# A hybrid decoder trunk on one core: the first two token blocks of the shared key projection move from the transposes' PSUM banks to the accumulator's

## The chip, the cores and the metric

The kernel runs on one core of one Trainium2 chip. The metric is the time of one execution on the device in microseconds (us), lower is better. The core's engines are PE (matrix products and transposes), DVE and POOL (vector work), ACT (activations and copies) and SP, which issues most of the transfers. Each engine works through its own queue in order. An instruction that waits for another engine holds up everything behind it on its queue.

## The reference, cut to what matters

The program computes a two-layer decoder trunk for one sequence of 512 tokens and a model width of 1024, in float32. Layer 0 has native sparse attention beside memory attention, and a squared-ReLU MLP. After it, keys and values are projected once from the residual stream. Layer 1 has dilated sliding-window attention over these keys and values beside memory attention, an output projection, and a second MLP. Cut to the part around the change:

```python
x = x + squared_relu_mlp(rmsnorm(x, mlp_norm[0]), w_up[0], w_down[0])   # end of layer 0
k_s, v_s = jnp.split(rmsnorm(x, kv_norm) @ w_kv_shared, 2, axis=-1)      # 512 x 1024 times 1024 x 1024
k_shared = rope(rmsnorm(split_heads(k_s, 8), kv_k_norm), pos)
v_shared = split_heads(v_s, 8)
q, q_mem = jnp.split(rmsnorm(x, attn_norm[1]) @ b_w_in[0], [B_Q], axis=-1)
o_main = dilated_attention(q, k_shared, v_shared, b_q_norm[0])           # three patterns, merged
o_mem = memory_attention(q_mem, mem_kv, mem_q_norm[1], mem_k_norm[1])
x = x + jnp.concatenate([o_main, o_mem], axis=-1) @ b_w_out[0]
```

## The kernel before, in words

**Products.** Each float32 operand is split into a high and a low part, so each product is three matmuls: high by high (L260), high by low (L261), low by high (L262). A pair of weight tiles is loaded into a staging buffer (pool `st`, 3 buffers) by a transfer on SP. ACT then copies the high part to a buffer of pool `w` (L253, 4 buffers), and DVE or POOL makes the low part by a subtraction (L255).

**PSUM.** The eight banks are four pools (L186): `acc` with 2 banks, `ps` with 3, `pt` with 2 and `po` with 1. A tile taken from a pool waits until the instructions that read the tile that had this bank before it are done. Names in the trace and in the order begin with the pool: `s_acc_6795` is a tile of `acc`, with its number.

**End of layer 0's MLP.** The last quarter of the MLP accumulates products in pairs of banks and adds them into the result `xn` (a tile of the SBUF pool `pt4`, shown as s_pt) with DVE (L216, in `into`). The last two steps are `product(X, ...)`, in the two `acc` banks, evicted by `into(X, 0, 0)`, and `product(V, ...)`, in the `pt` banks, evicted by `into(V, 0, 1)`. The result is in rows by tokens. `columns` (L1243 to L1265) turns it: for each half of the token rows and of the columns it takes a `ps` bank, makes four transposes of 128 x 128 per bank on PE (L1251), copies the bank out with ACT (L1258) or DVE (L1256), writes it to DRAM (`xd`), and builds the scaled operand `xk` of the key and value projection from it with ACT (L276) and DVE (L277). Token rows 256 to 511 are turned earlier, rows 0 to 255 in the very end of the MLP.

**Keys and values.** `layer_b` then calls `proj` (L300) for the keys, in the order of the token blocks 2, 3, 0, 1 (128 tokens each), so that the blocks whose operands are there first come first. One block is eight weight tiles by three matmuls of 128 x 512, in one bank. `proj` takes the bank where the block begins; its argument `pool` is one pool for all blocks, or a list that is indexed by the token block:

```python
ps = self.ps(pool[b] if isinstance(pool, list) else pool or self.pacc, [P, n])
```

Each finished key block is normalised on DVE (L513, L1419) and rotated on POOL (L524 to L527, L1423), in two halves. The value blocks follow in `ps` banks, evicted by ACT (L1404) and written to DRAM by POOL (L1405). Then come the query projections of layer B (`proj_b`).

**End of layer B's attention.** Memory attention runs there in four items (scores L657, softmax on ACT at L216, transposes L676, copies L730, values L734), beside the merge of the three dilated patterns (L1661 to L1681). The first part of the output projection, `outpart` (L1115 to L1149), fills the gaps on PE with blocks of nine matmuls into `acc` banks, each with its own weight (transfer from `in_w_bo_dram` to `st`, ACT L253, then L255). Its last part accumulates in `ps` banks when all heads are done.

**What sets the order.** The program text gives a first order. The scheduler of the framework then orders each engine's queue with a simulated timeline of the whole program (`schedule_with_timeline_sim=True`), so a change at one place can alter the order elsewhere.

## Time and profile before

| | |
|---|---|
| Runs | 1295.83, 1298.2 and 1300.5 us, median 1298.2 us |
| Profiled execution, its own time | 1296.08 us |
| Its span | 1294.3 us, 18328 instructions |
| Mean granted clock of PE | 0.995 |
| PE busy | 1244.8 us, 96% of the span |
| DVE, ACT, POOL busy | 825.1, 756.5 and 379.0 us (64%, 58%, 29%) |
| Last MLP matmul before the transposes of rows 0 to 255 | starts at 682.66 us |
| First matmul of the key projection | starts at 688.57 us |

The rows of the timeline that follow give the start and the duration of an instruction, its engine and line, what it writes and reads, the shape and the count; in square brackets stands how long the engine was idle just before it, and what it waited for. All times are counted from the start of the span.

### The profile page before, as it was taken

The numbers are of one execution on the slowest core, as the hardware profiler recorded it, in microseconds if no ns is written. First come the engines' busy times: TensorE is split into PE (matmuls) and PEld (weight loads), VectorE is DVE, ScalarE is ACT, GpSimd is POOL, SyncE is SP. The second block draws the span as 40 slices with busy tenths as digits, with TensorE's granted clock in tenths as the row PEclk, the third lists the DMA queues.
The fourth block names the chain that finished last, engine by engine and source line by source line (L and its number), as shares of the span: only waits on it lengthen the run. The fifth ranks groups of instructions, "written<-read, shape, count | busy, mean of one in ns | idle before, by whom it ended". The sixth has DMA issues, their size and how long they took to land.

```text
span 1294.3 us, 18328 instructions
## 1 busy us (share of the span) xinstructions
PE 1244.8 (96%) x6416; PEld 1021.6 (79%) x6416; DVE 825.1 (64%) x1502; ACT 756.5 (58%) x1684; POOL 379.0 (29%) x478
## 2 busy tenths in 40 slices
PE   9899989899999999999998989998999999999998
PEld 7768777677788888888887888887678888888887
DVE  6846676654656557465588467676657656656566
ACT  6845677774575464554657367777557445355462
POOL 4546665633140010000104689562314000000000
PEclk9999999999999999999999999999999999999999
DMA  7531231334488797887874421210339789697434
GB/s 260 195 119 55 67 126 62 66 74 132 159 252 234 248 238 231 276 237 248 236 212 139 143 74 51 71 42 9 108 126 291 219 271 243 211 287 218 151 110 163
DMA packets 61837, 215.28 MB, mean 166 GB/s; under 512 B 6736, under 2 KB 14928, under 8 KB 61232
## 3 DMA queue, kind: packets, MB, share of 16 engines
q1 hardware_dynamic: 50800, 143.72, 33.7%
q0 software_dynamic: 9344, 35.77, 14.0%
q10 hardware_dynamic: 1600, 34.61, 7.4%
q8 instruction: 51, 0.84, 0.3%
q14 instruction: 42, 0.34, 0.1%
HBM read 208.83 MB, written 72.35 MB: 217 GB/s over the span
## 4 chain that ended last, share of the span: by engine, by line
PE 80%; DVE 8%; ACT 6%; POOL 3%; issue 2%; DMA 2%; POOLq 0%; ACTq 0%; DVEq 0%
PE s_ps L261 14%; PE s_ps L262 13%; PE s_ps L260 13%; PE s_acc L260 5%; PE s_acc L261 5%; PE s_acc L262 5%; PE s_po L734 3%; PE s_pt L261 3%; PE s_pt L262 3%; PE s_pt L260 3%; DVE s_w L255 2%; ACT s_p L216 1%; PE s_ps L1542 1%; PE s_acc L867 1%; PE s_acc L566 1%
## 5 line engine op out<-in xcount | busy, mean ns | idle before, releaser
L255 DVE TENSOR_TENSOR s_w<-s_st,s_w 128x1024 fp32r<-128x1024 f32 (+3 forms) x228 | 272.0, 1197 | 254.7 <-ACT s_w L253 253.7
L253 ACT ACTIVATE s_w<-s_st 128x1024 fp32r<-128x1024 f32 (+4 forms) x260 | 251.3, 970 | 186.8 <-PE s_pt L262 41.1
L260 PE MATMUL s_ps<-s_act,s_w 128*128 128x512 f32 x568 | 222.1, 393 | 1.4 <-ACT s_act L295 1.4
L261 PE MATMUL s_ps<-s_act,s_w 128*128 128x512 f32 x568 | 221.4, 390 | 0.9 <-DVE s_act L1681 0.9
L262 PE MATMUL s_ps<-s_act,s_w 128*128 128x512 f32 x568 | 221.6, 390 | 0.0
L260 PEld LDWEIGHTS s_ps<-s_act,s_w 128*128 128x128 f32 x568 | 106.5, 188 | 25.2 <-ACT s_act L295 3.2
L261 PEld LDWEIGHTS s_ps<-s_act,s_w 128*128 128x128 f32 x568 | 106.7, 188 | 23.3 <-DVE s_act L1681 1.1
L262 PEld LDWEIGHTS s_ps<-s_act,s_w 128*128 128x128 f32 x568 | 106.6, 188 | 21.9
L216 ACT ACTIVATE s_p<-s_ps 128x512 f32<-128x512 f32 x64 | 38.2, 597 | 112.5 <-PE s_ps L262 112.5
L1170 POOL DMA_DIRECT2D sum<-in_w_db_dram x16 | 14.4, 902 | 295.3 <-ACT s_p L216 293.6
L260 PE MATMUL s_acc<-s_w,s_act 128*128 128x512 f32 (+3 forms) x272 | 94.9, 354 | 3.6 <-DVE s_tq L947 2.2
L261 PE MATMUL s_acc<-s_w,s_act 128*128 128x512 f32 (+3 forms) x272 | 95.1, 351 | 2.0 <-POOL s_w L255 1.8
L262 PE MATMUL s_acc<-s_w,s_act 128*128 128x512 f32 (+3 forms) x272 | 93.7, 350 | 0.0
L722 POOL TENSOR_SCALAR s_p<-s_p,s_cr,s_ab 128x128 f32<-128x128 f32 (+3 forms) x96 | 60.3, 664 | 47.9 <-DVE s_cr L1063 26.4
L255 POOL TENSOR_TENSOR s_w<-s_st,s_w 128x512 fp32r<-128x512 f32 (+4 forms) x32 | 54.6, 1706 | 63.6 <-ACT s_w L253 63.5
L216 ACT ACTIVATE s_p<-s_ps,s_nm 128x256 f32<-128x256 f32 (+3 forms) x128 | 65.5, 523 | 9.6 <-DVE s_nm L1043 2.8
L730 ACT ACTIVATE s_pt<-s_pt 128x512 f32<-128x512 f32 (+2 forms) x101 | 52.7, 525 | 20.6 <-PE s_pt L1087 8.5
L295 ACT ACTIVATE s_qk<-s_p 128x256 fp32r<-128x256 f32 (+1 forms) x96 | 47.0, 489 | 22.1 <-DVE s_p L1180 20.1
L260 PEld LDWEIGHTS s_acc<-s_w,s_act 128*128 128x128 f32 x272 | 51.7, 191 | 9.7 <-DVE s_tq L947 1.5
L1170 POOL DMA_DIRECT2D sum<-sum x16 | 14.1, 884 | 147.1 <-DMA sum<-sum 38.4
L261 PEld LDWEIGHTS s_acc<-s_w,s_act 128*128 128x128 f32 x272 | 51.9, 191 | 6.3 <-POOL s_w L255 2.4
L262 PEld LDWEIGHTS s_acc<-s_w,s_act 128*128 128x128 f32 x272 | 51.9, 191 | 3.6
(328 smaller groups left out, 2942.3 us busy)
## 6 DMA issues: line engine op xcount, KB each, us to landing
s_st<-in_w_up_dram SPq DMA_DIRECT2D x64, 512.0 KB, 4.1
s_st<-sum SPq DMA_DIRECT2D x64, 512.0 KB, 6.7
s_st<-in_w_db_dram SPq DMA_DIRECT2D x48, 512.0 KB, 4.5
sum<-in_w_db_dram POOLq DMA_DIRECT2D x16, 1024.0 KB, 13.9
sum<-sum POOLq DMA_DIRECT2D x16, 1024.0 KB, 10.9
s_st<-in_w_bq_dram SPq DMA_DIRECT2D x16, 384.0 KB, 3.1
s_st<-in_w_ag_dram SPq DMA_DIRECT2D x11, 512.0 KB, 3.9
s_w<-in_w_c_dram SPq DMA_DIRECT2D x8, 512.0 KB, 5.0
```

Source lines behind the costliest of these rows:

```text
L216: return lambda *a, **k: self.marks.append(f(*a, **k))
L253: nc.scalar.activation(w[:, 0], st, AF.Copy)
L255: e.tensor_tensor(out=w[:, 1], in0=st, in1=w[:, 0], op=ALU.subtract)
L260: mm(ps, lh[0], rh[0], start=start, stop=False, skip_group_check=again)
L261: mm(ps, lh[0], rh[1], start=False, stop=False, skip_group_check=again)
L262: mm(ps, lh[1], rh[0], start=False, stop=stop, skip_group_check=again)
L295: nc.scalar.activation(dst[:, 0], src, AF.Copy)
L566: nc.tensor.matmul(banks[b], tiles[k // 4][:, k % 4, b * P : (b + 1) * P], w[:, k % 4 // 2, k % 2 * 512 : k % 2 * 512 + 512], start=k == 0 ...
L722: self.nc.gpsimd.tensor_scalar(out=p, in0=p, scalar1=c, scalar2=g, op0=ALU.mult, op1=ALU.mult)
L730: self.turned = self.nc.scalar.activation(dst, src, AF.Copy)
L734: i = self.nc.tensor.matmul(*a, **k)
L1170: self.behind(self.nc.gpsimd.dma_start(t[o], x, accum_op=ALU.add, max_dma_last_dim=4096))
```

## The change

The argument `pool` of the key projection is a list now. Token blocks 2 and 3, which are computed first, take their banks from `acc`; blocks 0 and 1 take theirs from `ps` as before.

```diff
-        drain(self.proj(xk, ins["w_kv"][0], 512, evac_k, pool=self.pS, order=(2, 3, 0, 1)))
+        drain(
+            self.proj(xk, ins["w_kv"][0], 512, evac_k, pool=[self.pS, self.pS, self.pacc, self.pacc], order=(2, 3, 0, 1))
+        )
```

The number of instructions is the same on every engine but for how equal ones in a row are counted. Their order differs in two places. Lines behind the edit have a number that is higher by 2 after the change.

The first place is PE at the end of layer 0's MLP: transposes of the result (s_ps_6743 and 6755 are two of the `ps` banks, c_115 is the identity) and the start of the key projection (block tile 6795 and then 6867). Before:

```order
L1251 MATMUL s_ps_6743<-c_115,s_pt_1081_4072 128x128
L1251 MATMUL s_ps_6755<-c_115,s_pt_1081_4072 128x128
L1251 MATMUL s_ps_6755<-c_115,s_pt_1080_4071 128x128
L1251 MATMUL s_ps_6755<-c_115,s_pt_1081_4072 128x128
L260 MATMUL s_ps_6795<-s_w_6787,s_act_6572 128x512
L261 MATMUL s_ps_6795<-s_w_6787,s_act_6572 128x512
```

And now, from the last product of the first group to the next transpose:

```order
L262 MATMUL s_acc_6795<-s_w_6792,s_act_6589 128x512
L260 MATMUL s_acc_6795<-s_w_6804,s_act_6640 128x512
L260 MATMUL s_acc_6867<-s_w_6787,s_act_6572 128x512
L261 MATMUL s_acc_6867<-s_w_6787,s_act_6572 128x512
L262 MATMUL s_acc_6867<-s_w_6787,s_act_6572 128x512
L1251 MATMUL s_ps_6743<-c_115,s_pt_1080_4071 128x128
L260 MATMUL s_acc_6867<-s_w_6787,s_act_6575 128x512
```

The first product of block 6795 stood behind all sixteen transposes; it stands behind the second of them now, twelve more products of this block and the first three of block 6867 stand ahead of the first transpose into 6743, and the other transposes stand between further products.

The second place is ACT at the end of layer B's attention. There s_w_9754 and s_w_9788 are weights of the filler blocks, s_w_9883 and s_w_9895 weights of the last part of the output projection, and s_p_2185_9772 and s_p_2202_9828 are softmax rows of memory attention. Before:

```order
L253 ACTIVATE s_w_9788<-s_st_9786 128x384
L730 ACTIVATE s_pt_2158_9683<-s_pt_9684 128x2x256
L730 ACTIVATE s_pt_2158_9683<-s_pt_9727 128x2x256
L253 ACTIVATE s_w_9883<-s_st_9881 128x384
L253 ACTIVATE s_w_9895<-s_st_9893 128x384
L216 ACTIVATE s_p_2185_9772,s_su_9770<-s_ps_9764,s_nm_9769 128x256 x2
L730 ACTIVATE s_pt_2192_9795<-s_pt_9796 128x2x256
```

And now:

```order
L730 ACTIVATE s_pt_2158_9683<-s_pt_9684 128x2x256
L730 ACTIVATE s_pt_2158_9683<-s_pt_9727 128x2x256
L253 ACTIVATE s_w_9754<-s_st_9752 128x384
L216 ACTIVATE s_p_2185_9772,s_su_9770<-s_ps_9764,s_nm_9769 128x256 x2
L730 ACTIVATE s_pt_2192_9795<-s_pt_9796 128x2x256
L253 ACTIVATE s_w_9788<-s_st_9786 128x384
L1673 ACTIVATE s_p_2196_9804<-s_pt_9802 128x512
```

The copies of 9883 and 9895 stood ahead of the softmax row 9772 and stand further behind now; the copy of 9754, which stood further ahead, stands directly ahead of it, and that of 9788 behind it.

The third place is PE beside it, where s_acc_9757 and s_acc_9791 are the last two filler blocks of nine matmuls, s_pt_9796 and s_pt_9839 take transposes of softmax rows, and s_pt_9802 and s_pt_9807 belong to the merge. Before, both filler blocks stood wholly ahead of these rows:

```order
L262 MATMUL s_acc_9791<-s_act_9352,s_w_9788 128x512
L1661 MATMUL s_pt_9741<-idr,s_nb_9603 8x128 x4
L676 MATMUL s_pt_9796<-c_115,s_p_2169_9714 128x128 x4
L1669 MATMUL s_pt_9802<-s_p_2176_9746,s_ab_6782 128x512
L1674 MATMUL s_pt_9807<-s_p_2176_9746,s_ab_6782 128x512
L676 MATMUL s_pt_9839<-c_115,s_p_2185_9772 128x128 x4
L734 MATMUL s_po_9733<-s_pt_2128_9582,s_tmp_3258 64x512
```

And now, from the last product of filler 9757:

```order
L262 MATMUL s_acc_9757<-s_act_9352,s_w_9754 128x512
L1671 MATMUL s_pt_9802<-s_p_2176_9746,s_ab_6782 128x512
L1676 MATMUL s_pt_9807<-s_p_2176_9746,s_ab_6782 128x512
L260 MATMUL s_acc_9791<-s_act_8302,s_w_9788 128x512
L261 MATMUL s_acc_9791<-s_act_8302,s_w_9788 128x512
L676 MATMUL s_pt_9839<-c_115,s_p_2185_9772 128x128 x4
L262 MATMUL s_acc_9791<-s_act_8302,s_w_9788 128x512
```

Filler 9757 stands between the transposes of 9796 and the merge now, and filler 9791 around the transposes of 9839.

## The prediction

> **What bounds the kernel now.** I read the first part of the page, then the chain of waits, then the 2-us windows of busy time, then the timelines of the engines around the two places that the change touches. Start with the page:

> ```profile
> span 1294.3 us, 18328 instructions
> PE 80%; DVE 8%; ACT 6%; POOL 3%; issue 2%; DMA 2%; POOLq 0%; ACTq 0%; DVEq 0%
> ```

> Four fifths of the chain that ends last run through PE. So the kernel gets shorter where PE stands still or runs slowly, and only as far as nothing else is late there. The key projection begins in such a place. The windows (us, then busy time of PE, weight loads, DVE, ACT, POOL, then the granted clock, the DMA share and GB/s) show it:

> ```profile
> 682.00:684.00 2.00, 1.92 (x13) 1.48 (x11) 1.65 (x5) 1.97 (x7) 0.00 (x0) 1.00 0.89 322
> 684.00:686.00 2.00, 0.33 (x1) 0.14 (x1) 2.00 (x6) 2.00 (x4) 0.00 (x0) 1.00 0.97 286
> 686.00:688.00 2.00, 0.47 (x2) 0.29 (x3) 2.00 (x4) 2.00 (x5) 0.00 (x0) 1.00 0.23 94
> 688.00:690.00 2.00, 2.00 (x9) 1.72 (x9) 2.00 (x4) 2.00 (x6) 0.00 (x0) 0.60 1.01 238
> 690.00:692.00 2.00, 2.00 (x7) 1.57 (x6) 2.00 (x5) 2.00 (x7) 0.00 (x0) 0.55 0.96 340
> 692.00:694.00 2.00, 2.00 (x10) 1.69 (x9) 2.00 (x7) 2.00 (x7) 0.00 (x0) 1.00 1.03 388
> ```

> From 684 to 688 PE works 0.80 us of 4 while DVE and ACT are full; then it is full, but with a granted clock of 0.60 and 0.55. What it waits for stands in its timeline: the sixteen transposes of the MLP's result (L1251), and behind them on PE's queue the key projection's products (L260 to L262).

> ```profile
> 682.89 1.03 PE L1251 MATMUL s_ps<-c,s_pt 128*128 128x128 f32 x8
> 685.66 0.33 PE L1251 MATMUL s_ps<-c,s_pt 128*128 128x128 f32 x1 [1.74 <-DVE s_pt L216]
> 687.19 0.33 PE L1251 MATMUL s_ps<-c,s_pt 128*128 128x128 f32 x1 [1.19 <-ACT s_x L1258]
> 687.85 1.07 PE L1251 MATMUL s_ps<-c,s_pt 128*128 128x128 f32 x6 [0.34 <-DVE s_pt L216]
> 688.57 0.78 PE L260 MATMUL s_ps<-s_w,s_act 128*128 128x512 f32 x1
> ...
> 691.99 0.39 PE L262 MATMUL s_ps<-s_w,s_act 128*128 128x512 f32 x1
> ...
> 701.06 0.39 PE L260 MATMUL s_ps<-s_w,s_act 128*128 128x512 f32 x1
> ```

> PE waits 1.74, 1.19 and 0.34 us, 3.27 together, for the last MLP evictions and for a transpose bank. The first key product starts at 688.57, 0.86 behind the start of the copy on DVE that empties its bank:

> ```profile
> 680.23 0.75 DVE L216 SCALAR_TENSOR_TENSOR s_pt<-s_acc,r,s_pt 128x512 f32<-128x512 f32 x1
> ...
> 687.71 0.68 DVE L1256 COPY s_x<-s_ps 128x512 f32<-128x512 f32 x1
> ```

> The eviction that reads the MLP's own accumulator (s_acc) for the last time before this starts at 680.23 and takes 0.75. So those banks are empty from about 681 and idle, before the transposes begin. Those are the banks that the change takes.

> **The change part by part.** It adds and removes no instruction. The key products for token blocks 2 and 3 no longer stand behind all transposes: 48 of them (two blocks of eight weight tiles by three products) now stand among the transposes. Nothing else of the program text moves, but the scheduler simulates the whole program, so the order at the end of layer B's attention comes out differently too. I cost both.

> First place, the sum. Before, block 0, the third in order, begins at 701.06, which is 18.17 us behind the first of these transposes (701.06 - 682.89). Full-speed spacing comes from the 40 products between 691.99 and 701.06: 9.07 / 40 = 0.227. The first 8 took 691.99 - 688.57 = 3.42 where 8 x 0.227 = 1.82 would do, so the slow clock costs 1.6. Of the 18.17 us, then: 48 x 0.227 = 10.9 are products, 3.27 are waits, 1.6 is clock, and 2.4 are transposes and their beginnings. With the products between them PE has work at each of the three waits: ten products are there to run while DVE finishes the two L216 and the copy. Six transposes in a row need 688.57 - 687.85 = 0.72, or 0.12 each, so sixteen need 1.9. After the change I get 10.9 + 1.9 = 12.8, and the block begins at 695.7. The gain is 18.17 - 12.8 = 5.4 (5.35, rounded). It is bound by 0 from below (if another input keeps the products back as long as the bank did) and by 5.6 from above (3.27 + 1.6 + all but 1.7 of the transposes' 2.4).

> Are the other inputs there? The weights of the third and fourth pair go through ACT (high part) and DVE (low part), as the next rows show:

> ```profile
> 684.67 1.99 ACT L253 ACTIVATE s_w<-s_st 128x1024 fp32r<-128x1024 f32 x2
> 685.92 1.22 DVE L255 TENSOR_TENSOR s_w<-s_st,s_w 128x1024 fp32r<-128x1024 f32 x1
> 688.31 1.22 DVE L255 TENSOR_TENSOR s_w<-s_st,s_w 128x1024 fp32r<-128x1024 f32 x1
> 695.87 0.47 DVE L277 SCALAR_TENSOR_TENSOR s_act<-s_x,gv,s_act 128x256 fp32r<-128x256 f32 x1
> ```

> The low parts are ready at 687.14 and 689.53. By my walk through the new order PE wants the third pair at about 686.3 for its high part (ready at 685.7) and from 687 on for its low part, and the fourth at about 690. No wait is over a few tenths. The last input of the first token rows (L277) ends at 696.34, and those rows are wanted by block 0 alone, its pairs in turn from 695.7 to 701; the last pair is the late one, with over 3 us to spare. So I take 5.3 of 5.4 here.

> Does the gain survive what follows? The keys go through the rotary steps on POOL, and POOL then makes the low parts of the query weights:

> ```profile
> 697.09 0.73 POOL L524 TENSOR_TENSOR s_rb<-s_x,c 128x256 f32<-128x256 f32 x1 [51.58 <-DVE s_r L228]
> ...
> 726.78 0.62 POOL L1423 TENSOR_TENSOR s_x<-s_x,s_r 128x256 f32<-128x256 f32 x1
> ...
> 731.68 1.84 POOL L255 TENSOR_TENSOR s_w<-s_st,s_w 128x768 fp32r<-128x768 f32 x1 [1.61 <-ACT s_w L253]
> 733.70 0.51 PE L260 MATMUL s_ps<-s_w,s_act 128*128 128x384 f32 x2
> ...
> 737.55 0.44 PE L261 MATMUL s_ps<-s_w,s_act 128*128 128x384 f32 x1 [1.23 <-DVE s_w L255]
> ```

> The chain from 697.09 to 727.40 is busy without a break and begins with a DVE step whose place on its queue hardly changes (about 0.5 earlier). It therefore ends at about 726.9, while PE arrives 5.3 earlier. POOL's first weight then would end near 729.3 if it follows right behind the keys; PE took it up at 733.70, so 5.3 earlier it wants it near 728.6, waits about 0.7, and then finds the wait of 1.23 at 737.55 shorter by as much. That nets to nothing, and 5.3 is kept. If the chain were the bound with no such slack, the loss would be all of 5.3; this is the second rival.

> Second place, the end of layer B's attention. Its rows on PE, of the timeline:

> ```profile
> 931.31 0.50 PE L1669 MATMUL s_pt<-s_p,s_ab 8*128 8x512 f32 x1 [0.69 <-DVE s_p L1665]
> 932.68 0.50 PE L1674 MATMUL s_pt<-s_p,s_ab 8*128 8x512 f32 x1 [0.87 <-ACT s_pt L730]
> ...
> 933.98 3.55 PE L734 MATMUL s_po<-s_pt,s_tmp 128*64 128x512 f32 x8
> ...
> 940.20 0.50 PE L261 MATMUL s_ps<-s_act,s_w 128*128 128x512 f32 x1 [0.91 <-DVE s_act L1681]
> ...
> 943.82 1.94 PE L734 MATMUL s_po<-s_pt,s_tmp 128*64 128x512 f32 x8
> 946.46 0.98 PE L260 MATMUL s_ps<-s_act,s_w 128*128 128x512 f32 x3 [0.70 <-ACT s_act L295]
> ```

> Four waits, 0.69 + 0.87 + 0.91 + 0.70 = 3.17. And two groups of eight equal products: 3.55 against 1.94, so 1.6 of clock, which the windows confirm:

> ```profile
> 934.00:936.00 2.00, 2.00 (x7) 0.65 (x8) 0.88 (x4) 2.00 (x8) 1.49 (x2) 0.54 0.16 54
> 936.00:938.00 2.00, 2.00 (x7) 0.51 (x4) 1.07 (x2) 0.69 (x2) 2.00 (x4) 0.61 0.24 62
> ```

> By these it is (1 - 0.54) x 2 + (1 - 0.61) x 2 = 1.7. Together 4.9. The second wait is named for L730, but ACT stood behind a weight that had not landed, with the softmax (L216) queued behind it:

> ```profile
> 928.17 2.45 DMA s_st<-in_w_bo_dram
> 930.71 0.52 ACT L253 ACTIVATE s_w<-s_st 128x384 fp32r<-128x384 f32 x1 [0.73 <-DMA s_st<-in_w_bo_dram]
> 931.14 0.46 ACT L216 ACTIVATE s_p<-s_ps,s_nm 128x256 f32<-128x256 f32 x1
> ```

> In the new order the two copies of output weights that stood ahead of this softmax (9883, 9895) stand behind it, and one that is needed sooner (9754) stands there instead; two filler blocks of nine products stand between the transposes and merges at which PE waited; and four products stand behind the last L734 where PE had waited 0.70 for L295. Walking the new order with the old durations, I get the trio of 946.46 at 940.2, 6.3 earlier, with waits of 0.15 and 0.4 left. The bounds are 6.3 above, and below a small loss, since later copies also free the staging buffers 1.0 to 1.5 later. I take 5, near the 4.9 of the quoted rows, because a walk by hand omits waits that only show when the order runs.

> From 740 to 905 the order on the engines is the same but for a row or so, and what stands there waits for PE, so I carry the shift through at no cost.

> The sum: 5.3 + 5.0 = 10.3, taken as 10. Against the profiled execution, 1296.1 - 10 = 1286.1. That execution lies 2.1 under the median of the runs shown (1298.2), so against the median I expect **1288.2**.

> [...]

> **The rivals.** *Only the first place counts.* For it: the second rests on a walk through an order, and each removed wait there can come back at the next eviction (0.91 at L1681 stays in part). Against: its causes are quoted rows, and the order takes them away. It would give 5.3: 1298.2 - 5.3 = 1293.

> *POOL's key chain takes the first gain back.* For it: the chain has no breaks from 697.09 to 727.40, and the query weights stand behind it. Against: there are 4.3 us between its end and the start at 731.68, and that start waits for ACT. It would leave the 5 of the second place: 1293.

> *The clock terms are not saved.* For it: the dip moves to another idle stretch, as 930 to 934 shows that 1.1 to 1.2 us of work in 2 can be enough. Against: both stretches become full. The gain is 10.3 - 1.6 - 1.7 = 7.0: 1291.

> *Nothing is gained.* The products among the transposes delay the transposes, and so the rows that all 24 products of block 0 need, by as much as PE gained, and the end nets to zero. For it: DVE and ACT are full from 684 to 694, and every window shows 2.00. Against: they work off a backlog that does not hang on PE; the walk leaves over 3 us. 1297 to 1298. That the change doesn't do what it says is excluded by the order, where the products name the accumulator's banks.

> *Slower.* Mechanism: the output weights at the end of the attention become the pacing chain. With three staging buffers, ACT's in-order copies stand at four places ahead of other work (9754, 9788, 9907, 9931), and each is freed 1.0 to 1.5 later than before. The landing there is measured:

> ```profile
> s_st<-in_w_bo_dram SPq DMA_DIRECT2D x13, 192.0 KB, 2.3
> s_st<-sum SPq DMA_DIRECT2D x64, 512.0 KB, 6.7
> ```

> To come out slower by 3.9 it must cost 10.3 + 3.9 = 14.2 over my walk, or 3.6 at each of the four, a landing of 5.9 instead of 2.3. The MLP's slowest class needs 6.7, but for 512 KB. From that point the time is 1302.

> **How the numbers follow.** Both places, near 1288: 0.56. The clock not saved, 1291: 0.12. Only the first place: 0.12. Only the second: 0.07. Nothing: 0.09. Slower: 0.04. A difference of 0.3%, 3.9 us, is about what a measurement of this kernel tells from none. The first four all lie beyond it, though the two at 1293 only by 1.3, of which I count 0.03 as no change: faster 0.84, same 0.12, slower 0.04. The range: below, both upper bounds, 5.6 + 6.3 = 11.9, off the lowest run shown (1295.8) give 1283.9, so 1284; above, the cases at 1293 with 2.3 more, which is the scatter of the runs around their median, 1295.5. About 0.15 is left out.

> **What would show it.** In the changed profile the first key product starts before 685 into an accumulator bank, the 48 run at 0.227 with a clock near 1.00 in the windows from 684 to 694, and block 0 starts near 695.7. If it starts after 697.5, the first term is wrong. POOL's rotary steps still begin near 697, and the wait at the query weights stays under 1 us. At the end of the attention the L1674 wait for L730 is gone, the eight L734 take 1.9, and the trio of three L260 comes about 11 us earlier than 946.46 (5.3 + 6). If ACT's L253 waits for a landing longer than 1 us with L216 behind it, the second term is wrong. A time over 1295.5 would make the whole wrong, since then one of the two gains came back in full.

## The result, and the profile after

The changed kernel takes 1287.74 us in the median of 6 runs (1285.92 to 1289.99), against 1295.9 us of 6 runs of the kernel before (1294.27 to 1300.5). The ratio is 0.9923, with a 95% interval of 0.9903 to 0.9943, so 7 to 13 us less. 1288.2 us was predicted, as 10 us off a median of 1298.2 (three runs). Over all runs whose clock is on record the medians are 1297.3 (54 runs of the kernel before, without the six above) and 1288.9 us (19 runs of the changed one, with its six).

The profiled execution has a span of 1286.8 us, and PE has a smaller part of the chain of waits than before (76% against 80%). The first rows are the page's, as shown of the kernel before:

```profile
span 1286.8 us, 18330 instructions
PE 76%; DVE 8%; ACT 7%; DMA 3%; POOL 3%; issue 2%; POOLq 0%; ACTq 0%; DVEq 0%
```

The windows of the changed kernel around the start of the key projection (us, then busy time of PE, weight loads, DVE, ACT, POOL, then granted clock, DMA share, GB/s). Everything stands 2.4 us earlier here than in the first profile of before. That lies ahead of the change, most of it (1.5) between 100 and 200 us, where the kernel before has a stretch of half clock in that profile:

```profile
680.00:682.00 2.00, 2.00 (x14) 1.75 (x13) 1.65 (x5) 2.00 (x6) 0.00 (x0) 1.00 1.04 297
682.00:684.00 2.00, 2.00 (x10) 1.61 (x9) 2.00 (x4) 2.00 (x5) 0.00 (x0) 1.00 0.54 215
684.00:686.00 2.00, 2.00 (x11) 1.62 (x10) 2.00 (x3) 1.97 (x5) 0.00 (x0) 1.00 0.45 102
686.00:688.00 2.00, 2.00 (x13) 1.62 (x13) 2.00 (x6) 2.00 (x7) 0.00 (x0) 1.00 0.92 321
688.00:690.00 2.00, 2.00 (x12) 1.70 (x11) 2.00 (x8) 2.00 (x6) 0.00 (x0) 1.00 0.94 363
```

PE is full and its clock is 1.00 in all of them, where it had 0.33 and 0.47 of 2 us in two windows and then a clock of 0.60 and 0.55. Its timeline shows why: the products stand among the transposes, and none of the rows has a wait.

```profile
680.46 0.38 PE L1251 MATMUL s_ps<-c,s_pt 128*128 128x128 f32 x2
680.59 0.48 PE L260 MATMUL s_acc<-s_w,s_act 128*128 128x512 f32 x1
680.91 0.82 PE L1251 MATMUL s_ps<-c,s_pt 128*128 128x128 f32 x6
...
687.53 0.82 PE L1251 MATMUL s_ps<-c,s_pt 128*128 128x128 f32 x6
...
693.21 0.39 PE L260 MATMUL s_ps<-s_w,s_act 128*128 128x512 f32 x1
```

The third block starts 693.21 - 680.46 = 12.75 us behind the first of these transposes; it was 18.17. The second stop is the hand-over to layer B's query projection. There the third value block's copy on ACT, and behind it PE, wait (rows of ACT, POOL and PE):

```profile
721.63 0.69 ACT L1404 ACTIVATE s_raw<-s_ps,rt 128x512 f32<-128x512 f32 x1 [0.88 <-DMA vd<-s_raw]
719.15 0.61 POOL L1405 DMA_DIRECT2D vd<-s_raw  x1
726.76 0.45 PE L261 MATMUL s_ps<-s_w,s_act 128*128 128x384 f32 x1 [0.41 <-POOL s_w L255]
730.74 0.44 PE L261 MATMUL s_ps<-s_w,s_act 128*128 128x384 f32 x1 [1.59 <-DVE s_w L255]
```

PE waits 2.0 us where it had waited 1.23 (and not at all in the second and third profile of before). The third is the end of layer B's attention. The eight equal products take 1.94 us from the start, and in place of the four waits (3.17 us) there are two, 2.24 us together. L1682 and L1683 are L1680 and L1681 of the kernel before, so the second is what is left of a wait of 0.91, and the first is new and longer than any of the four:

```profile
927.31 1.94 PE L734 MATMUL s_po<-s_pt,s_tmp 128*64 128x512 f32 x8
...
931.61 0.70 PE L260 MATMUL s_ps<-s_act,s_w 128*128 128x512 f32 x2 [1.66 <-DVE s_act L1682]
...
933.21 0.73 PE L261 MATMUL s_ps<-s_act,s_w 128*128 128x512 f32 x2 [0.58 <-DVE s_act L1683]
```

But the slow clock has not gone. Three stretches of half clock stand elsewhere in this execution:

```profile
863.45:866.86 3.41, 3.41 (x17) 3.41 (x18) 1.74 (x3) 1.69 (x8) 3.04 (x4) 0.50 0.00 0
873.69:877.10 3.41, 3.41 (x18) 3.41 (x17) 1.34 (x3) 1.27 (x4) 1.44 (x2) 0.50 0.01 2
897.58:900.99 3.41, 3.41 (x19) 1.96 (x19) 1.85 (x3) 1.78 (x7) 2.21 (x3) 0.50 0.01 2
```

To see where time goes I matched the same PE instructions of every profile with those of the first profile of before. The table gives by how much each part of the program, named by its times in that profile, took longer (+) or shorter (-), in us, and where the stretches of half clock lay (each 3.41 us; the end of the program is left out).

| Kernel (profile) | 683 to 701, first place | 701 to 760, hand-over | 760 to 869 | 869 to 950, end of attention | Half clock from |
|---|---|---|---|---|---|
| before | 0 | 0 | 0 | 0 | 173, 688, 934 |
| before, 2nd | +0.5 | -0.1 | 0.0 | -0.1 | 174, 689, 754, 935 |
| before, 3rd | +0.3 | -0.2 | -0.1 | -0.1 | 687, 751, 932 |
| changed | -5.4 | +1.1 | 0.0 | -0.7 | 54, 863, 874, 898 |
| changed, 2nd | -5.4 | +1.9 | 0.0 | -2.2 | 172, 749, 896 (twice as long) |
| changed, 3rd | -5.4 | +2.1 | 0.0 | -0.9 | 173, 866, 876, 900 |
| changed, 4th | -5.4 | +1.8 | 0.0 | -1.5 | 56 (twice as long), 284, 868, 878, 902 |

The first place gives what was predicted. The hand-over takes 1.1 to 2.1 back. (In the second and third profile of before PE has no wait there, which is 1.5 us less, and pays it to the stretch of half clock at 754 or 751, 1.3 to 1.5 us.) The end of the attention gives 0.7 to 2.2, not 5.

### The profile page after: what moved, and what is told of

The parts are those of the page before. It is cut to its first block, busy times and chain, and to the rows that moved or that the text cites. A ratio compares the mean times of both kernels' runs of the same rounds, so it can differ in the third digit from the quotient of the medians.

```text
span 1286.8 us, 18330 instructions
## 1 busy us (share of the span) xinstructions
PE 1244.2 (97%) x6416; PEld 1022.9 (79%) x6416; DVE 827.3 (64%) x1502; ACT 756.2 (59%) x1684; POOL 377.8 (29%) x478
## 4 chain that ended last, share of the span: by engine, by line
PE 76%; DVE 8%; ACT 7%; DMA 3%; POOL 3%; issue 2%; POOLq 0%; ACTq 0%; DVEq 0%
PE s_ps L262 13%; PE s_ps L261 13%; PE s_ps L260 13%; PE s_acc L260 5%; PE s_acc L261 5%; PE s_acc L262 5%; PE s_po L734 3%; PE s_pt L262 3%; PE s_pt L260 3%; PE s_pt L261 3%; ACT s_p L216 2%; DVE s_w L255 2%; PE s_acc L867 1%; PE s_ps L1544 1%; PE s_acc L566 1%
## 5 line engine op out<-in xcount | busy, mean ns | idle before, releaser
L255 DVE TENSOR_TENSOR s_w<-s_st,s_w 128x1024 fp32r<-128x1024 f32 (+3 forms) x228 | 272.1, 1198 | 254.5 <-ACT s_w L253 253.7
L253 ACT ACTIVATE s_w<-s_st 128x1024 fp32r<-128x1024 f32 (+4 forms) x260 | 251.4, 970 | 189.7 <-PE s_pt L262 46.2
L260 PE MATMUL s_ps<-s_act,s_w 128*128 128x512 f32 x568 | 221.7, 392 | 2.4 <-DVE s_act L1682 1.7
L261 PE MATMUL s_ps<-s_act,s_w 128*128 128x512 f32 x568 | 221.3, 390 | 0.6 <-DVE s_act L1683 0.6
L262 PE MATMUL s_ps<-s_act,s_w 128*128 128x512 f32 x568 | 221.7, 391 | 0.0
L260 PEld LDWEIGHTS s_ps<-s_act,s_w 128*128 128x128 f32 x568 | 106.5, 188 | 25.3 <-ACT s_w L253 1.9
L262 PEld LDWEIGHTS s_ps<-s_act,s_w 128*128 128x128 f32 x568 | 106.6, 188 | 23.0 <-issue 0.8
L261 PEld LDWEIGHTS s_ps<-s_act,s_w 128*128 128x128 f32 x568 | 106.6, 188 | 22.9 <-DVE s_act L1683 0.8
L260 PE MATMUL s_acc<-s_w,s_act 128*128 128x512 f32 (+3 forms) x288 | 102.4, 361 | 2.9 <-DVE s_tq L947 1.5
L216 ACT ACTIVATE s_p<-s_ps 128x512 f32<-128x512 f32 x64 | 38.2, 597 | 112.6 <-PE s_ps L262 112.6
L261 PE MATMUL s_acc<-s_w,s_act 128*128 128x512 f32 (+3 forms) x288 | 102.2, 357 | 2.0 <-POOL s_w L255 1.7
L262 PE MATMUL s_acc<-s_w,s_act 128*128 128x512 f32 (+3 forms) x288 | 100.4, 354 | 0.0
L216 ACT ACTIVATE s_p<-s_ps,s_nm 128x256 f32<-128x256 f32 (+3 forms) x128 | 65.4, 522 | 12.1 <-DVE s_nm L1043 3.1
L255 POOL TENSOR_TENSOR s_w<-s_st,s_w 128x512 fp32r<-128x512 f32 (+4 forms) x32 | 54.8, 1713 | 51.7 <-ACT s_w L253 51.7
L730 ACT ACTIVATE s_pt<-s_pt 128x512 f32<-128x512 f32 (+2 forms) x101 | 52.7, 525 | 18.9 <-PE s_pt L1087 7.0
L260 PEld LDWEIGHTS s_acc<-s_w,s_act 128*128 128x128 f32 x288 | 55.7, 194 | 9.7 <-DVE s_tq L947 1.6
L261 PEld LDWEIGHTS s_acc<-s_w,s_act 128*128 128x128 f32 x288 | 55.8, 194 | 6.9 <-POOL s_w L255 2.3
L295 ACT ACTIVATE s_qk<-s_p 128x256 fp32r<-128x256 f32 (+1 forms) x96 | 46.9, 489 | 22.1 <-DVE s_p L1180 20.1
L262 PEld LDWEIGHTS s_acc<-s_w,s_act 128*128 128x128 f32 x288 | 55.7, 194 | 4.2
## 6 DMA issues: line engine op xcount, KB each, us to landing
s_st<-in_w_up_dram SPq DMA_DIRECT2D x64, 512.0 KB, 4.3
s_st<-sum SPq DMA_DIRECT2D x64, 512.0 KB, 6.5
s_st<-in_w_db_dram SPq DMA_DIRECT2D x48, 512.0 KB, 4.4
s_st<-in_w_ag_dram SPq DMA_DIRECT2D x11, 512.0 KB, 4.0
s_w<-in_w_c_dram SPq DMA_DIRECT2D x8, 512.0 KB, 4.8
```

The source lines that it names most:

```text
L216: return lambda *a, **k: self.marks.append(f(*a, **k))
L253: nc.scalar.activation(w[:, 0], st, AF.Copy)
L255: e.tensor_tensor(out=w[:, 1], in0=st, in1=w[:, 0], op=ALU.subtract)
L260: mm(ps, lh[0], rh[0], start=start, stop=False, skip_group_check=again)
L261: mm(ps, lh[0], rh[1], start=False, stop=False, skip_group_check=again)
L262: mm(ps, lh[1], rh[0], start=False, stop=stop, skip_group_check=again)
```

## The experiments

The kernel before and the changed one were profiled again, with no edit.

> The kernel before, nothing left out, for a second profile. Theory (the stretches of half clock fall on idle time by chance of the execution, not on the two places alone): three to five stretches of 3.41 us, not all at 173, 688 and 934 us; around the places that have none the kernel is up to 1.7 us faster than in the first profile. Rival (they belong to the two places): again 173, 688 and 934.

> The kernel before a third time, as before_again: theory, the stretches of half clock move again; rival, 173, 688 and 934 us once more. Waits of PE between 682 and 689 us are 3.2 to 3.4 us in every profile by both.

They took 1296.73 and 1294.26 us. PE's waits ahead of the key projection were 3.8 and 3.6 us, a little more than expected. The stretches of half clock came back at the two places, in the second profile and in the third (windows of the one, then of the other):

```profile
689.24:692.66 3.42, 3.42 (x11) 2.75 (x10) 3.42 (x7) 3.42 (x10) 0.00 (x0) 0.50 0.93 287
935.00:938.42 3.42, 3.42 (x10) 0.96 (x7) 1.61 (x5) 2.28 (x8) 3.24 (x4) 0.50 0.22 51
```

```profile
686.58:690.00 3.42, 3.42 (x12) 2.93 (x11) 3.42 (x7) 3.42 (x10) 0.00 (x0) 0.50 0.95 263
932.34:935.76 3.42, 3.42 (x10) 0.77 (x7) 1.72 (x5) 2.19 (x8) 3.13 (x4) 0.50 0.11 21
```

So the rival was right for these two: they belong to the places. The others (173, and 751 or 754) come in some executions. Just ahead of the latter PE stands still for 2.3 us in every profile of both kernels, a wait that the prediction does not name (first profile of before, then of the change):

```profile
754.72 0.70 PE L755 MATMUL s_pt<-idr,s_qki 128*128 128x128 f32 x6 [2.34 <-DVE s_qki L698]
747.93 0.70 PE L755 MATMUL s_pt<-idr,s_qki 128*128 128x128 f32 x6 [2.36 <-DVE s_qki L698]
```

> The changed kernel once more, nothing left out. Theory: the gain over the kernel before is again about 8 us (7 to 10). In its profile the key projection's third block starts 12.7 to 12.9 us behind the first transpose, PE waits about 1 us for the query weights near 727 to 731, and the stretches of half clock, each 3.41 us long, lie at other places than in the first profile (there: 54, 863, 874 and 898 us). Rival (the three stretches at 863, 874 and 898 are caused by the new order): they come back at the same three places.

> The changed kernel a third time. Theory: two to five stretches of half clock, none between 680 and 700 us, since PE has no idle time there; third block 12.7 to 12.9 us behind the first transpose; PE's waits for the query weights 1.2 to 2.0 us in all. Rival (the stretches belong to the order of the end of the attention): at 863, 874 and 898 us.

> The changed kernel a fourth time, as the measure for the other kernels of this call. Theory: 7 to 11 us faster than before; of it about 6 at equal clock and the rest because fewer stretches of half clock fall on it (mean granted clock 0.995 to 0.996 against 0.992 to 0.993 before, each 0.001 worth about 1.1 us). Rival (the clock plays no part in the mean gain): equal mean clocks, and a gain of 6.

The 2nd took 1289.13 us (ratio 0.9914, 0.9889 to 0.9938), the 3rd 1290.91 in one run, the 4th 1288.81 (0.9941, 0.9924 to 0.9959). In none of the four profiles is there a slow stretch between 680 and 700, and the third block starts 12.7 to 12.8 us behind the first transpose in each. The stretches near 863 and 874 came back in the 3rd and 4th profile, not in the 2nd; one near 900 came in all four. Neither theory nor rival holds as written: the place near 900 belongs to this kernel, the pair ahead of it to some executions.

The mean granted clock of each of these runs is on record. Over the 54 runs of before it is 0.9925, over the 19 of the change 0.9953. Clock loss, taken as (1 - clock) x time, is 9.8 and 6.0 us. Within the 54 runs of before, time rises by 0.82 us for each us of it (correlation 0.90). By that, 0.82 x 3.75 = 3.1 of the 9.4 us between the means (1297.8 and 1288.4) go with the clock, and 6.3 remain at equal clock. In the table that follows, times at a clock of 0.995 are worked out in this way.

| Kernel | Runs | Median | Ratio to before (95%) | Mean clock | Mean time at 0.995 |
|---|---|---|---|---|---|
| before | 54 | 1297.3 | | 0.9925 | 1295.0 |
| changed | 19 | 1288.9 | 0.9914, 0.9923 and 0.9941, measured three times | 0.9953 | 1288.7 |
| all four key blocks in acc | 12 | 1297.3 | 0.9984 (0.9965 to 1.0003) | 0.9928 | 1294.6 |
| blocks 2 and 3 in pt | 12 | 1290.1 | 0.9947 (0.9925 to 0.9968) | 0.9936 | 1289.8 |
| block 2 alone in acc | 8 | 1290.8 | 0.9951 (0.9934 to 0.9968) | 0.9938 | 1289.2 |
| change, value writes on SP | 6 | 1290.6 | 0.9933 (0.9910 to 0.9956) | 0.9950 | 1290.2 |
| change, query low parts on DVE | 12 | 1293.2 | 0.9965 (0.9948 to 0.9983) | 0.9904 | 1288.6 |
| change, first low part on DVE | 7 | 1290.2 | 0.9941 (0.9920 to 0.9963) | 0.9933 | 1287.2 |
| the same, value writes on SP | 6 | 1287.0 | 0.9929 (0.9912 to 0.9946) | 0.9918 | 1284.3 |

**Block 2 alone.**

```diff
-pool=self.pS, order=(2, 3, 0, 1)
+pool=[self.pS, self.pS, self.pacc, self.pS], order=(2, 3, 0, 1)
```

> Only token block 2, the first, accumulates in the accumulator's bank; block 3 goes to a bank of the transposes as before. The order at the end of layer B's attention is the change's. Theory (24 products, 5.4 us, are enough to cover waits of 3.3 us in all): third block 12.7 to 13.2 us behind the first transpose, no stretch of half clock behind it, the time of the change within 1 us. Rival (both blocks are needed, because the second one's bank is freed only by the last copies): PE waits 1 to 2 us ahead of block 3, third block at 14 to 15, 1 to 2 us slower than the change.

Block 3 follows the last transposes without a wait (rows of PE):

```profile
688.45 0.93 PE L1251 MATMUL s_ps<-c,s_pt 128*128 128x128 f32 x7
689.13 0.48 PE L260 MATMUL s_ps<-s_w,s_act 128*128 128x512 f32 x1
```

The third block starts 12.8 us behind the first transpose and the first place gains 5.3 us, as in the change. One block of 24 products is enough cover. In time this kernel is 2 us behind the change measured beside it, with intervals that overlap; its profile has the hand-over at +3.1, of which 1.5 is a slow stretch at 751.

**Blocks 2 and 3 in the banks of the very last MLP product.**

```diff
-pool=self.pS, order=(2, 3, 0, 1)
+pool=[self.pS, self.pS, self.pT, self.pT], order=(2, 3, 0, 1)
```

> Blocks 2 and 3 accumulate in the two banks that the very last MLP product leaves, which are evicted last, instead of those of the product before it. The order at the end of layer B's attention is as in the change. Theory (what counts is that the bank is free early): the first key product cannot start before the last two evictions, about 2.8 us after the first transpose, the third block starts about 14.6 us behind the first transpose instead of 12.75, or up to 1.7 more if the clock drops in the idle time; the 1 us lost at the query weights is hidden. About 1 us slower than the change, 7 us faster than before. Rival (any bank but those of the transposes will do): third block at 12.8, the time of the change. Rival (all from the end of the attention): the same time as the change although the first place is as in the kernel before.

The first transposes start at 679.52 here. The first product stands behind the eviction that empties its bank (on DVE, 681.16 to 681.90), as the theory had it, and the third block comes at 693.83, 14.3 us behind (14.6 expected, 12.75 in the change):

```profile
681.96 0.33 PE L1251 MATMUL s_ps<-c,s_pt 128*128 128x128 f32 x1 [1.41 <-DVE s_pt L216]
682.05 0.48 PE L260 MATMUL s_pt<-s_w,s_act 128*128 128x512 f32 x1
...
693.83 0.39 PE L260 MATMUL s_ps<-s_w,s_act 128*128 128x512 f32 x1
```

So it counts when the bank comes free, not only that it is another one. The 1.5 us that this place loses against the change are not lost at the end: PE waits nowhere at the hand-over, which with a slow stretch at 746 comes to 0.0 instead of 1.1 to 2.1. From 683 on this profile is 7.9 us ahead of before, the four of the change 4.3 to 5.8, with one slow stretch at the end of the attention against two or three. PE came later to a hand-over that was late anyway.

**All four key blocks in the accumulator's two banks.** In this build the order at the end of the attention is that of the kernel before.

```diff
-pool=self.pS, order=(2, 3, 0, 1)
+pool=self.pacc, order=(2, 3, 0, 1)
```

> All four key blocks accumulate in the two banks of the accumulator pool. The order at the end of layer B's attention comes out as in the kernel before, so this is the first place alone. Theory (both places gain): the first two blocks start as early as in the change; block 0 then waits for the eviction of block 2 on DVE, which ends about 2 us after PE wants the bank, so 3.3 of the 5.4 stay; the 1 us that the change loses at the query weights is not lost on top; the end of the attention gains nothing but chance clock. Sum 3 to 4 us faster than before, about 4.5 us slower than the change. Rival (the whole gain is made at the first place and the end of the attention gives nothing): 6 to 7 us faster than before, within 2 of the change.

It was not clearly faster than before (0.9965 to 1.0003, in the middle 2 us), where 3 to 4 were expected. The wait for block 2's bank was 2.77 us (DVE empties it with L1419, at 697.46 to 697.87, and the row names the instruction behind that), and half clock followed it (rows of PE, then windows):

```profile
698.01 0.47 PE L260 MATMUL s_acc<-s_w,s_act 128*128 128x512 f32 x1 [2.77 <-DVE s_r L513]
```

```profile
696.00:698.00 2.00, 0.00 (x0) 0.02 (x1) 1.97 (x7) 1.50 (x6) 1.45 (x2) 1.00 0.00 0
698.00:700.00 2.00, 1.99 (x6) 1.62 (x7) 1.93 (x8) 1.60 (x7) 1.85 (x4) 0.66 0.00 0
700.00:702.00 2.00, 2.00 (x6) 1.51 (x6) 1.62 (x5) 0.80 (x3) 1.84 (x4) 0.50 0.00 0
```

The first place gained only 2.5. The slow stretch behind it took 1.5 of these and another one at 753, which two profiles of before have too, 1.4. This run says what a late bank costs (its wait, and the clock behind it), and less on what I wanted from it. The end of the attention was 0.05 us off the kernel before, with the same stretch at 934. That does agree with a gain there that comes from the order.

**The first query weights' low parts all on DVE.** The order around the key projection is the change's, that at the end of the attention is the kernel before's.

```diff
-        yield from self.proj(xg, ins["w_bq"][sp], 384, evac, pool=pool, lo="gv", delay=delay)
+        yield from self.proj(xg, ins["w_bq"][sp], 384, evac, pool=pool, lo="gv" if sp else "v", delay=delay)
```

> The change, with the low parts of the first query projection's weights all made on DVE instead of alternately on POOL and DVE. In this build the order on PE around the key projection is the change's but for two rows, and the order at the end of layer B's attention is that of the kernel before; between them some rows move. So it is the first place alone, with another hand-over to the query projection. Theory (two separate gains, 3.8 without clock at the first place, 3.3 at the end of the attention): third block 12.7 to 12.9 us behind the first transpose; PE's waits at the end of the attention are the four of the kernel before (3.2 us together); total 4 to 5.5 us faster than before, about 4 slower than the change. Rival (the end's order matters for nothing, its gain in the first trace was chance): 7 to 9 us faster, as the change.

It was 4 to 5 us faster than before (0.9965) and 4 behind the median of all runs of the change (2.3 behind the one run measured beside it), which the theory expected. The waits at the end are back (rows of PE):

```profile
931.83 0.50 PE L1671 MATMUL s_pt<-s_p,s_ab 8*128 8x512 f32 x1 [0.68 <-DVE s_p L1667]
933.11 0.50 PE L1676 MATMUL s_pt<-s_p,s_ab 8*128 8x512 f32 x1 [0.78 <-ACT s_pt L730]
```

Yet the account is another than the one expected. From 701 to 760 this kernel gained 2.1 instead of losing, though not at the hand-over (+0.3): the wait of 2.34 us at L755 is gone. From 760 to 869 5.1 us were lost, with four periods of half clock in the profile between 765 and 851. At equal clock this kernel stands beside the change (1288.6), with a gain that the change has not, so its time alone does not prove that the end's order is worth anything.

**The value writes on SP instead of POOL.**

```diff
-            nc.gpsimd.dma_start(vd[b * P : (b + 1) * P, :], t)
+            nc.sync.dma_start(vd[b * P : (b + 1) * P, :], t)
```

> The change, with the four writes of the value blocks to DRAM issued by SP instead of POOL; the order on PE, ACT and DVE is that of the change. Theory (the changed kernel gives 1.05 us back because the writes stand behind the key rotation on POOL's queue, so that the third value block's copy on ACT waits for its buffer, and the query operands and weights behind it): that wait of 0.88 on ACT is gone, the waits of PE for the query weights shrink from 0.41 + 1.59 to about 1.2 in all, and the kernel is 1 us faster than the change. Rival (POOL's own weight step is late anyway): the waits move to the subtraction on POOL, no gain. Rival (SP's queue): the writes stand behind weight loads that wait for a staging buffer, the copy waits longer, and the kernel is 1 to 3 us slower than the change.

The wait on ACT is gone. But the eight builds of the query operand on DVE (L277) took 7.21 us instead of 5.4, and PE waits 1.54 for the weight behind them (rows of ACT, DVE and PE):

```profile
723.22 0.67 ACT L1404 ACTIVATE s_raw<-s_ps,rt 128x512 f32<-128x512 f32 x1
724.32 7.21 DVE L277 SCALAR_TENSOR_TENSOR s_act<-s_x,gv,s_act 128x256 fp32r<-128x256 f32 x8 [0.50 <-ACT s_act L276]
732.45 0.44 PE L261 MATMUL s_ps<-s_w,s_act 128*128 128x384 f32 x1 [1.54 <-DVE s_w L255]
```

No gain: 1290.64 us, against 1289.13 of the change measured beside it. The second wait was hidden behind the first.

**The first low part on DVE, without and with the writes on SP.** Each has the edit shown, the second one also that of the writes:

```diff
-lo="gv", delay=delay)
+lo="gv" if sp else "vvgv", delay=delay)
```

> The change, and of the four weight loads of the first query projection the low part of the first is made on DVE instead of POOL (third still on POOL). Order on PE around the key projection and at the end of the attention is the change's. Theory (the change gives 0.7 to 2.1 us back at this hand-over because POOL comes out of the key rotation late, and because DVE and POOL slow each other there): PE's wait for the first low part is gone; waits between 720 and 740 us 0.7 or less; 1 us faster than the change. Rival (ACT's third value copy, which waits for POOL's write, sets the pace): waits as in the change, same time.

> As the kernel with the first low part on DVE, and the value blocks' writes issued by SP instead of POOL as well. Theory (both causes act together at the hand-over, each hidden behind the other when removed alone): no wait of PE over 0.3 us between 720 and 740 us, 1.5 to 2.5 us faster than the change at equal clock, and the fastest kernel of all. Rival (PE's gain there is given back behind, as where an early hand-over was followed by a stretch of half clock near 750 us): waits gone, time as the change.

The waits went as expected: one of 0.47 us is left in the first kernel between 720 and 740, and none in the second. On DVE each low part took 0.94 to 0.98 us in the second, and the one that POOL still makes ended 731.7:

```profile
726.61 0.94 DVE L255 TENSOR_TENSOR s_w<-s_st,s_w 128x768 fp32r<-128x768 f32 x1
```

```profile
729.28 2.44 POOL L255 TENSOR_TENSOR s_w<-s_st,s_w 128x768 fp32r<-128x768 f32 x1 [2.88 <-ACT s_w L253]
```

From 701 to 760 they are 2.8 and 3.9 us shorter than before, so 3.9 to 6.0 shorter than the change. But 2.4 of this is not the hand-over. In these two kernels, as in the one with all low parts on DVE, the order on DVE is another: L698 stands ahead of a low part that stood ahead of it, and PE's wait at L755 is gone (rows of DVE and PE, the first profile of the change, then the second kernel):

```profile
744.06 2.55 DVE L255 TENSOR_TENSOR s_w<-s_st,s_w 128x768 fp32r<-128x768 f32 x1 [1.48 <-ACT s_w L253]
746.53 1.34 DVE L698 TENSOR_TENSOR s_qki<-s_tq,s_qki 128x384 fp32r<-128x384 f32 x1
```

```profile
743.13 0.59 DVE L698 TENSOR_TENSOR s_qki<-s_tq,s_qki 128x384 fp32r<-128x384 f32 x1 [1.22 <-ACT s_qki L697]
744.23 2.01 DVE L255 TENSOR_TENSOR s_w<-s_st,s_w 128x768 fp32r<-128x768 f32 x1
744.92 0.63 PE L755 MATMUL s_pt<-idr,s_qki 128*128 128x128 f32 x6
```

The hand-over itself, up to 745, is 0.4 and 1.5 us shorter than before, where the change is 0.7 to 2.1 longer. From 760 to 869 they lose 6.2 and 3.7, with four and three stretches of half clock (windows of the second):

```profile
763.70:767.10 3.40, 3.40 (x12) 3.40 (x11) 2.05 (x5) 2.21 (x3) 3.32 (x4) 0.50 0.00 0
825.10:828.50 3.40, 3.40 (x13) 3.40 (x12) 0.80 (x2) 1.31 (x6) 3.40 (x5) 0.50 0.00 0
842.20:845.60 3.40, 3.33 (x15) 3.33 (x16) 3.40 (x6) 3.00 (x9) 3.37 (x4) 0.50 0.40 139
```

PE's idle time there is 0.8 us more than before in the first and 0.3 less in the second. The rest, 5.4 over four stretches and 4.0 over three, is 1.3 or 1.4 for each, which is within 1.7, an estimate of the most that a clock of 0.50 takes of 3.41 us. So the rival of the last expectation, that the gain is given back behind, holds for most of it. In time the first kernel is 1.4 us behind the change measured beside it (1290.24 against 1288.81), where 1 us ahead was expected, and the second is 1.8 us ahead (1287.03), with intervals that overlap. It is the fastest by its median and by its time at equal clock (1284.3), but that it beats the change in time is not shown.

## Why the prediction was right, and where it was not

The time (1288.2 predicted, 1287.7 measured) was right, and so was the direction. That the two agree within 0.5 us is in part luck: the gain was put at 10 and is 8.2 beside the six runs of before, whose median is 2.3 us under that of the three runs from which the forecast counted. Of its two terms the first was right in size and in mechanism, the second was too large in the clock that it was to save, and a loss was missed.

**First place, 5.4.** Measured 5.42, 5.41, 5.42 and 5.41 in four profiles. The third block was put at 12.8 us behind the first transpose and came at 12.75. The parts hold too. The waits are gone, the stretch of half clock at this place stood in all three profiles of before and in none of the change, and the banks' early eviction is the cause: with banks that come free later the gain fell to 3.9.

**Hand-over.** The step that failed is "That nets to nothing, and 5.3 is kept". It took 1.1 to 2.1 us. The first wait came nearly as put (0.41 for about 0.7), but the second, which was to shrink below 1.23, is 1.59. I had put POOL's chain at 726.9 and it ended at 724.32, with the profile's shift of 2.4 at 726.75, so the chain was right. What I left out are the four value writes that POOL issues (L1405): they stand behind the key rotation, the value copy on ACT needs the buffer that the first of them frees, and the query operand and its weights stand behind that copy on ACT. This wait is in the rows shown (0.88 on ACT). The run without it shows that it was not the only cause, since another one took its place. With the writes and POOL's first weight both moved, PE waited there no more. So the second rival, that POOL's chain takes the first gain back, happened for 1.1 to 2.1 of the 5.4, and not by POOL's chain alone.

**End of the attention, 5.** The waits quoted from before fell as predicted, but a new one came at L1682, and with the rest of the old one at L1683 it makes 2.24 us in the first profile, where my walk had left 0.15 and 0.4. Compared at an equal number of slow stretches (one, as in before, for which two other kernels with this order stand in the profiles), the place gains 3.9 us, near the 3.3 that were meant without the clock. The clock term, 1.7, is the one that was mis-sized. The stretch at 934 went, but one near 900 stood in all four profiles of the change, and in two or three windows of half clock from 863 on the place lost what it had won. "Both stretches become full" was right for these two stretches, and no reason for the clock to be saved. The third rival (the dip moves to another idle stretch) is what happened here. The clock terms also took in only the two stretches at these places: the first profile of before has a third, at 173 (and one at its end). And from 930 to 934, ahead of the second, PE was busy for 2.4 of 4 us, against 0.80 ahead of the first, so half clock also came behind half as much idle time (1.6 us against 3.2).

**The clock as a whole.** At equal clock the change is worth 6.3 us: by the profiles 5.4 less 1.6 at the first place, 3.9 at the end, less 1.7 at the hand-over, which is 6.0. Without its clock terms the sum had 7.0. The other 3.1 come from the mean clock, 0.9953 against 0.9925, where the sum had 1.6 and 1.7. The stretch at the first place, which no profile of the change has, can be half of these 3.1. Where the rest comes from the profiles don't show: the three profiled executions of before had clocks of 0.994 to 0.995 and were among the better ones, and those of the change have as many stretches or more. So that the clock as a whole gave about what the sum had for it is luck as to the second term, and the source of that half stays open.

The signs that I named for the first term all came. The wait at the query weights, which was to stay under 1 us, is 2.0. Of the signs for the second, the wait of L1674 for L730 is gone and the eight products take 1.94, but the trio of three L260 came at 939.07, 7.4 us earlier than before and not 11, and 2.4 of the 7.4 lie ahead of the change. The sign against the second term came too: ACT waited 1.86 us for a weight's landing, with a merge step (L1673) and softmax rows (L216) behind it:

```profile
923.97 0.52 ACT L253 ACTIVATE s_w<-s_st 128x384 fp32r<-128x384 f32 x1 [1.86 <-DMA s_st<-in_w_bo_dram]
```

## What to carry to other kernels

Where a product waits behind transposes for a bank, look which bank was emptied first and is idle: here one block of products in it was enough to cover the waits, and a bank that came free 2.4 us behind the first transpose still gave 3.9 of the 5.4. Follow the engine that was hidden until now through every queue that it feeds, the writes that it issues too. Where an edit alters the order elsewhere, look for waits that came or went far from it before the gain is put down to the edit. A gain that consists of granted clock should be counted at nothing until several executions show that the slow stretch does not turn up elsewhere.

## What the runs showed of the hardware

DVE or POOL took longer where each made a low part at the same time. One of 128x768 took DVE 0.94 us while POOL stood still (at 726.61 in the second kernel with the first low part on DVE), and two of them 3.44 in the first profile of the change, where POOL made one meanwhile (2.07). In the second profile of the change one took DVE 0.95 beside one that took POOL 2.93. The same step took POOL 1.8 to 2.2 us in the sixteen rows of the first profiles of before and of the change, and up to 2.96 elsewhere (blocks 2 and 3 in pt); DVE was at work in part of each of them, so what POOL takes alone is not shown.
